# The Mamba-2 stage of a hybrid encoder layer: in-chunk products with the values as weights, states of the second direction first, outputs finished chunk by chunk in feature-major layout

## The chip, the cores and the metric

The kernel runs on one core of one Trainium2 chip. The metric is the device time of one launch in microseconds. TensorE (PE) multiplies, VectorE (DVE), ScalarE (ACT) and GpSimd (POOL) work elementwise, and the queues of SyncE (SP) and ScalarE issue the DMAs. Every engine takes its instructions in order. On TensorE a product of plain fp32 operands is two passes; in the profile each pass is one weight load (PEld) and one MATMUL.

## The reference

One layer: RMSNorm, one input projection (1024 to 10016 columns), three branches (Mamba-2 SSD, RWKV-7, HGRN2), a gated merge, an output projection, and a SwiGLU FFN. L = 1024 positions, all fp32. The change lies in the Mamba-2 branch: 16 heads of 64 values, 2 groups of 8 heads that share B and C of 128 states, chunks of 128 positions, two directions with decays of their own, summed:

```python
a_cum = jnp.cumsum(dt * a, axis=2)                       # within a chunk
lmat = jnp.exp(jnp.where(mask, a_cum[q] - a_cum[s], -inf))
cb = einsum('bcqgn,bcsgn->bcqsg', cm, bm)
y_diag = einsum('bcqsgh,bcsghp->bcqghp', cb[..., None] * lmat, x * dt)
chunk_states = einsum('bcsgn,bcsghp->bcghpn', bm, x * dt * exp(a_cum[-1] - a_cum))
# scan over chunks: S <- exp(a_cum[-1]) * S + chunk_states, prev = S before the chunk
y_off = einsum('bcqgn,bcghpn->bcqghp', cm, prev) * exp(a_cum)
y = y_forward + y_backward + x * d_skip
out = rmsnorm(y * silu(z), norm_w)                       # over all 1024 features
```

## The kernel before, in words

The layer runs rwkv, hgrn, `ssd`, then merges, output projection and FFN. The input projection is a list of jobs (`Jobs`), one for each tile of 128 columns, of 16 steps of three matmuls each (L329 to L331, `mm<-x`); `J.fill` and `J.share` put steps between the work of the branches, so that TensorE has something to do while the other engines prepare operands. `J.share(w)` issues that part of the remaining steps which weight `w` (from the list `FILL["ss"]`, called F) has in the remaining `J.weight`. The number of steps is the same whatever the weights are. Each job also casts and splits its weights (`wh` on ScalarE L220, `wl` on VectorE L222) and copies its result from PSUM and stores it (`st`, L271 and L272, on ScalarE and its queue). The tiles of z (`pz`) are jobs, as are the gates (`pg`), which are last.

`ssd` has two groups of 8 heads. For each, B, C and x are convolved (L1285 to L1289), the products CB of B and C are made for all chunks, and x is transposed so that positions are on the partitions (`xt`). Then a loop over i = 0 to 7 treats chunk i of the first direction and chunk 7 - i of the second:

- `pairs(c)` makes the in-chunk matrix of chunk c for 8 heads, 128 x 1024: for each direction a load that copies rows of cumulated decay (`cumd`) to all partitions (512 KB, in one of the EB = 5 buffers with tag E), a subtraction on POOL (L1357), then the choice between the directions by a mask (L1360, VectorE), exp (L1361, ScalarE) and the product with CB (L1362, VectorE). It runs two chunks ahead.
- For each direction: `yo`, the product of C with the state S (L1378, one matmul with 512 moving columns), scaled into `yt` (L1380) and added to Y on POOL (L1381); `xw`, the weighted values (L1384); `st`, their product with B (L1386); the state update, decay on POOL (L1390) and sum on VectorE (L1391).
- `yd`, the in-chunk products (L1397): for each head the 128 x 128 matrix as weights and 64 value columns as moving operand; the result is added to Y (L1399).
- Y starts as xt times `gd`, on POOL (L1371). `gd` holds the skip term and a diagonal term.

After the loop the group loads its four tiles of z, takes silu (L1408), transposes Y to features on partitions (`ytps`, L1417), multiplies (L1418), stores (`ysc`, L1419), and adds the squares to `ss` (L1425, L1426), which the last norm needs in the merge.

The order of the work on every engine but one is set by a planner, which takes what is ready in its own model of time, earlier program text first. POOL in the chunk loop keeps the program's order (`tc.manual_schedule(engines={POOL})`). Buffers of one tag are reused only when their last reader is through; DMAs of SP are issued in order, and one that waits holds back those behind it.

## Time and profile before

| | before |
|---|---|
| median of three runs | 2487.82 us (2487.3 to 2491.13) |
| profiled execution | 2489.66 us, its span 2487.9 us |
| busy share PE / DVE / ACT / POOL | 94% / 66% / 40% / 43% |
| granted TensorE clock, mean | 0.964 |
| bytes moved by DMA | 306.27 MB |
| chunk loop of the first group | about 1183 to 1283 us of the span |
| chunk loop of the second group | about 1376 to 1483 us |

Times in the answers are microseconds from the start of the span. A group of instructions is given by line, engine, operation and tiles (written <- read) with its shape and count, then busy time and mean duration of one in ns, then idle time of the engine before them and what ended it. The duration of a matmul reaches over the next one, since they are pipelined; the pace is read from one start to the next.

### The profile page before, as it was taken

Reading aid. Unit: us, or ns where it says so; the run is one execution under the profiler, and the core shown is the slowest. Engines: PE = TensorE matmul, PEld = TensorE weight load, DVE = VectorE, ACT = ScalarE, POOL = GpSimd, SP = SyncE. Lnnn points to the kernel's source line nnn. Section 1 sums busy time; section 2 is a strip of 40 time slices with the busy share of each in tenths; the row PEclk is TensorE's granted clock in tenths of the full one; section 3 lists DMA queues with packets and bytes.
Section 4 is the critical chain, followed back from the end, with each engine's and each line's share of the span. In section 5 each row is a group of like instructions: output and inputs, shape, how many; then the busy total and the mean of one; then the engine's idle time right before and its main releaser. Section 6 shows DMA issues by size and latency. Waiting matters only on the chain.

```text
span 2487.9 us, 37793 instructions
## 1 busy us (share of the span) xinstructions
PE 2332.5 (94%) x14785; PEld 1870.3 (75%) x14785; DVE 1635.9 (66%) x2130; ACT 988.9 (40%) x1460; POOL 1068.9 (43%) x862
## 2 busy tenths in 40 slices
PE   8998999999989889999899899999899999999995
PEld 6776788888867677778568667788688888877764
DVE  5688862456566866846666776553774454469999
ACT  6544532222464653436135235332433333344333
POOL 4433422344044533420751761421454444447885
PEclk9998999899999999999899999999999999999998
DMA  5455685655342232225645647531132222253321
GB/s 149 126 145 131 164 209 139 189 164 149 118 138 91 77 109 77 68 88 172 140 125 172 142 128 250 189 115 72 60 102 81 80 84 78 85 172 109 102 67 68
DMA packets 381215, 306.27 MB, mean 123 GB/s; under 512 B 111273, under 2 KB 323149, under 8 KB 381037
## 3 DMA queue, kind: packets, MB, share of 16 engines
q1 hardware_dynamic: 260909, 225.71, 30.6%
q10 hardware_dynamic: 119936, 77.61, 10.7%
q8 instruction: 117, 1.92, 0.3%
q0 software_dynamic: 192, 0.52, 0.1%
q14 instruction: 61, 0.50, 0.1%
HBM read 209.68 MB, written 94.11 MB: 122 GB/s over the span
## 4 chain that ended last, share of the span: by engine, by line
PE 59%; DVE 23%; POOL 5%; issue 5%; DMA 4%; ACT 3%; SPq 0%; ACTq 0%; DVEq 0%; POOLq 0%
PE mm L329 6%; PE mm L330 6%; PE mm L331 6%; PE ps L1577 6%; PE ps L1576 6%; PE ps L1578 6%; DVE acc L1915 3%; DVE ab L1793 2%; PE Gps L802 2%; PE mm L232 2%; PE mm L230 2%; PE mm L231 2%; DMA E<-cumd 2%; POOL E L1357 2%; DVE rb L1793 2%
## 5 line engine op out<-in xcount | busy, mean ns | idle before, releaser
L329 PE MATMUL mm<-x,wh 128*128 128x512 f32 (+1 forms) x1232 | 500.0, 406 | 0.5 <-ACT wh L220 0.5
L330 PE MATMUL mm<-x,wh 128*128 128x512 f32 (+1 forms) x1232 | 497.2, 404 | 0.0
L331 PE MATMUL mm<-x,wl 128*128 128x512 f32 (+1 forms) x1232 | 495.0, 402 | 0.8 <-DVE wl L222 0.7
L329 PEld LDWEIGHTS mm<-x,wh 128*128 128x128 f32 (+1 forms) x1232 | 234.5, 190 | 62.2 <-issue 10.6
L331 PEld LDWEIGHTS mm<-x,wl 128*128 128x128 f32 (+1 forms) x1232 | 234.7, 190 | 57.2 <-issue 6.0
L330 PEld LDWEIGHTS mm<-x,wh 128*128 128x128 f32 (+1 forms) x1232 | 234.8, 191 | 55.9 <-issue 6.8
L1577 PE MATMUL ps<-xb,rb 128*128 128x512 f32 x432 | 171.1, 396 | 0.0
L1576 PE MATMUL ps<-xb,rb 128*128 128x512 f32 x432 | 170.1, 394 | 0.0
L1578 PE MATMUL ps<-xb,rb 128*128 128x512 f32 x432 | 169.9, 393 | 0.0
L220 ACT CAST wh<-wr 128x1024 fp32r<-128x1024 f32 (+2 forms) x103 | 100.3, 974 | 125.1 <-PE mm L330 102.4
L222 POOL TENSOR_TENSOR wl<-wr,wh 128x1024 fp32r<-128x1024 f32 x30 | 78.2, 2606 | 149.2 <-ACT wh L220 140.0
L1576 PE MATMUL ps<-rb,ab 128*128 128x512 f32 x308 | 127.4, 414 | 14.3 <-DVE acc L1915 13.5
L222 DVE TENSOR_TENSOR wl<-wr,wh 128x1024 fp32r<-128x1024 f32 (+2 forms) x73 | 98.1, 1343 | 64.6 <-ACT wh L220 64.5
L1577 PE MATMUL ps<-rb,ab 128*128 128x512 f32 x308 | 125.3, 407 | 2.3 <-POOL rb L1793 2.3
L1578 PE MATMUL ps<-rb,ab 128*128 128x512 f32 x308 | 124.1, 405 | 1.5 <-DVE ab L1793 1.5
L1740 ACT CAST rb<-fs 128x512 fp32r<-128x512 f32 x85 | 52.5, 621 | 172.1 <-PE ps L1578 119.7
L271 ACT COPY st<-mm 128x512 f32<-128x512 f32 x130 | 75.5, 581 | 95.1 <-PE mm L331 76.0
L805 DVE TENSOR_TENSOR Gc<-Gps,mk 128x256 f32<-128x256 f32 x64 | 27.0, 423 | 112.4 <-PE Gps L802 58.6
L1576 PEld LDWEIGHTS ps<-xb,rb 128*128 128x128 f32 x432 | 81.2, 188 | 19.9
L1578 PEld LDWEIGHTS ps<-xb,rb 128*128 128x128 f32 x432 | 81.2, 188 | 19.0
L1577 PEld LDWEIGHTS ps<-xb,rb 128*128 128x128 f32 x432 | 81.1, 188 | 18.9
L1357 POOL TENSOR_TENSOR E<-E,cums 128x1024 f32<-128x1024 f32 x32 | 68.3, 2146 | 60.3 <-DMA E<-cumd 54.5
(503 smaller groups left out, 5584.8 us busy)
## 6 DMA issues: line engine op xcount, KB each, us to landing
wr<-in_w_in_dram ACTq DMA_DIRECT2D x74, 512.0 KB
fr<-in_ffn_w_in_dram SPq DMA_DIRECT2D x44, 512.0 KB
E<-cumd SPq DMA_DIRECT2D x32, 512.0 KB
pg<-st ACTq DMA_DIRECT2D x48, 256.0 KB
gt<-pg SPq DMA_DIRECT2D x24, 512.0 KB
ad<-a SPq DMA_DIRECT2D x22, 512.0 KB
dr<-in_ffn_w_down_dram SPq DMA_DIRECT2D x22, 512.0 KB
ar<-ad SPq DMA_DIRECT2D x22, 512.0 KB
```

Of the source, the lines that this page charges most:

```text
L220: nc.scalar.copy(hi[:, :kt, :n], raw[:, :kt, :n])
L222: g.lo_eng.tensor_sub(lo[:, :kt, :n], raw[:, :kt, :n], f32(hi[:, :kt, :n]))
L271: g.nc.scalar.copy(st[:n], ps)
L329: g.nc.tensor.matmul(ps[:n], w[0][:, k, :n], xh, start=(k == 0), stop=False)
L330: g.nc.tensor.matmul(ps[:n], w[0][:, k, :n], xl, start=False, stop=False)
L331: g.nc.tensor.matmul(ps[:n], w[1][:, k, :n], xh, start=False, stop=(k == KT - 1))
L1357: nc.gpsimd.tensor_tensor(e, e, cs.unsqueeze(2).broadcast_to([P, 8, P]), SUB)
L1576: nc.tensor.matmul(ps, ah, bh, start=(i == 0), stop=False)
L1577: nc.tensor.matmul(ps, ah, bl, start=False, stop=False)
L1578: nc.tensor.matmul(ps, al, bh, start=False, stop=(i == n - 1))
L1793: eng.tensor_sub(blk[:, 1], s, f32(blk[:, 0]))
L1915: nc.vector.tensor_add(m[j], m[j], ps)
```

## The change

- `yd`: the values `xt` (64 columns) are now the weights and the matrix `e` is the moving operand (128 columns), so that outputs come feature-major; the two heads of a 128-feature tile write the two halves of the partitions.
- `yo`: four products for each direction, the state's 128-column pieces as weights, C as the moving operand, also feature-major.
- The factor exp(a_cum) is no longer a table (`ecum`), but computed from the broadcast rows: X = Exp(e), in two instructions of 64 partitions for each direction, on ScalarE.
- The sign of `cums` is turned; for the first direction the addition to e is eight ScalarE instructions with a bias, for the second it stays one instruction on POOL.
- The diagonal and the skip term are put in the matrix by a second predicated copy on VectorE (`id8`, `gd`) in place of the POOL product that began Y.
- States of the second direction for all chunks come first (`Sb`, seven steps), and then a loop over chunks that finishes each: y = both X products + `yd`, times z, stored to `ysc`, square on ScalarE, square sums on POOL.
- z of the group is loaded, given silu and stored to a DRAM buffer `zd` ahead of the loop, through buffers of tag E, and reloaded chunk by chunk.
- The transposes `ytps` and the end-of-group work go. FILL weights are set anew: total 543 in place of 551.

The diff, cut to its core:

```diff
-    "ss": (4, 36, 12, 18, 6, 3, 8, 5, 22, 13, 8),
+    "ss": (4, 36, 14, 5, 7, 8, 22, 13, 6),
...
-    J.weight = F[8] + 2 * F[0] + F[9] + F[10] + 2 * (F[1] + 4 * F[2] + F[3] + 16 * F[4] + 8 * F[5] + F[6] + 4 * F[7])
+    J.weight = F[6] + 2 * F[0] + F[7] + F[8] + 2 * (F[1] + 4 * F[2] + 7 * F[3] + 8 * F[4] + 8 * F[5])
...
-            nc.vector.tensor_sub(cums, cums, ld)
+            nc.vector.tensor_sub(cums, ld, cums)
...
+                for q in range(grp * 4, grp * 4 + 4):
+                    zs = sp.tile([P, L + 4], F32, tag="E", name="zs", bufs=EB)[:, :L]
+                    nc.sync.dma_start(zs, J.get(g.pz, q))
+                    nc.scalar.activation(zs, zs, AF.Silu)
+                    nc.sync.dma_start(zd[q], zs)
...
                 def pairs(c):
-                        nc.gpsimd.tensor_tensor(e, e, cs.unsqueeze(2).broadcast_to([P, 8, P]), SUB)
+                        X = yp.tile([P, 4, P], F32, tag=f"X{d}", name="X", bufs=2)
+                        if c != (0, NT - 1)[d]:
+                            for b in range(2):
+                                hr = slice(b * 64, b * 64 + 64)
+                                nc.scalar.activation(X[hr], e[hr, b::2], AF.Exp)
+                        if d == 0:
+                            for h in range(8):
+                                nc.scalar.activation(e[:, h], e[:, h], AF.Identity, bias=cums[:, c, h0 + h:h0 + h + 1])
+                        else:
+                            nc.gpsimd.tensor_tensor(e, e, cums[:, c, h0:h0 + 8].unsqueeze(2).broadcast_to([P, 8, P]),
+                                                    ADD)
...
                     nc.vector.tensor_mul(e, e, CB[:, c:c + 1, :].broadcast_to([P, 8, P]))
+                    nc.vector.copy_predicated(e, id8.unsqueeze(1).broadcast_to([P, 8, P]),
+                                              gd[:, c].unsqueeze(2).broadcast_to([P, 8, P]))
...
+                def state(d, c, old, new):
+                    xw = yp.tile([P, 512], F32, tag="xw", name="xw", bufs=2)
+                    nc.vector.tensor_tensor(h3(xw), h3(xt[:, c]), per_head(wst, c, d), MUL)
+                    ps = pp.tile([P, 512], F32, tag="b", name="st", bufs=2)
+                    nc.tensor.matmul(ps, Bt[:, c], xw, start=True, stop=True)
+                    if old is None:
+                        nc.vector.tensor_copy(new, ps)
+                    else:
+                        nc.gpsimd.tensor_tensor(h3(new), h3(old), per_head(dec, c, d), MUL)
+                        nc.vector.tensor_add(new, new, ps)
...
-                nxt = [pairs(0), pairs(1)]
+                nxt = [pairs(0)]
+                for c in range(NT - 1, 0, -1):
+                    state(1, c, Sb[:, c] if c < NT - 1 else None, Sb[:, c - 1])
+                    J.share(F[3])
+                nxt.append(pairs(1))
                 for i in range(NT):
+                    z = yp.tile([P, 4, P], F32, tag="z", name="z", bufs=2)
+                    nc.sync.dma_start(z, zd[grp * 4:grp * 4 + 4, :, ts].rearrange("q p t -> p q t"))
+                    e, X = nxt.pop(0)
+                    part = []
+                    for d, S in ((1, Sb[:, i] if i < NT - 1 else None), (0, Sa if i else None)):
+                        if S is None:
+                            continue
+                        ps = pp.tile([P, 4, P], F32, tag="b", name="yo", bufs=2)
+                        for q in range(4):
+                            nc.tensor.matmul(ps[:, q], S[:, q * P:(q + 1) * P], CT[:, ts], start=True, stop=True)
+                        nc.vector.tensor_mul(X[d], X[d], ps)
+                        part.append(X[d])
+                    if i < NT - 1:
+                        state(0, i, Sa if i else None, Sa)
+                    J.share(F[4])
                     for h in range(8):
-                        nc.tensor.matmul(ps[:, h], e[:, h], xt[:, i, h * 64:h * 64 + 64],
+                        nc.tensor.matmul(ps[h % 2 * 64:h % 2 * 64 + 64, h // 2], xt[:, i, h * 64:h * 64 + 64], e[:, h],
                                          start=True, stop=True)
+                    y = part[0]
+                    if len(part) > 1:
+                        nc.gpsimd.tensor_add(y, y, part[1])
+                    nc.vector.tensor_add(y, y, ps)
+                    nc.vector.tensor_mul(z, z, y)
+                    nc.sync.dma_start(ysc[grp * 4:grp * 4 + 4, :, ts].rearrange("q p t -> p q t"), z)
+                    nc.scalar.activation(y, z, AF.Square)
+                    eng = nc.vector if grp and i == NT - 1 else nc.gpsimd
+                    eng.tensor_add(y[:, 0:2], y[:, 0:2], y[:, 2:4])
+                    if grp == 0:
+                        eng.tensor_add(ss[:, ts], y[:, 0], y[:, 1])
+                    else:
+                        eng.tensor_add(y[:, 0], y[:, 0], y[:, 1])
+                        eng.tensor_add(ss[:, ts], ss[:, ts], y[:, 0])
+                    if i + 2 < NT:
+                        nxt.append(pairs(i + 2))
                     J.share(F[5])
-                for q in range(4):
-                    zs = zss[q]
-                    for h in range(2):
-                        ps = pp.tile([P, 4, P], F32, tag="a", name="ytps", bufs=3)
...
```

More of the change, by code (lines that the diff above doesn't have):

```diff
@@ L1212, in ssd @@
         cums = kp.tile([P, NT, 32], F32, tag="cums", name="cums")
-        ecum = kp.tile([P, NT, 32], F32, tag="ecum", name="ecum")
         wst = kp.tile([P, NT, 32], F32, tag="wst", name="wst")
@@ L1228, in ssd @@
             nc.vector.tensor_scalar(dA, dt, an[:, 0:1], None, MUL)
-            J.share(F[8])
+            J.share(F[6])
             dtT = kp.tile([P, NT, 32], F32, tag="dtT", name="dtT")
@@ L1258, in ssd @@
             nc.scalar.activation(dec, pse, AF.Exp)
-            nc.scalar.activation(ecum, cums, AF.Exp)
             nc.vector.tensor_sub(wst, pse, cums)
@@ L1273, in ssd @@
                                 base=-1, channel_multiplier=1)
-        m8 = kp.tile([P, P], U8, tag="m8", name="m8")
+        m8, id8 = (kp.tile([P, P], U8, tag=n, name=n) for n in ("m8", "id8"))
         nc.vector.tensor_copy(m8, mlt)
+        nc.vector.tensor_copy(id8, g.ident)
         def conv(ct, dst):
@@ L1303, in ssd @@
                 conv(10 + grp, CT)
-                J.share(F[1] + F[9] * grp)
+                J.share(F[1] + F[7] * grp)
                 cbd = yp.tile([P, NT], F32, tag="cbd", name="cbd")
@@ L1343, in h3 @@
                     return t.rearrange("p (h v) -> p h v", v=64)
-                S = [yp.tile([P, 512], F32, tag=f"S{d}", name=f"S{d}") for d in range(2)]
-                J.share(F[3])
                 def pairs(c):
-                    Es = []
+                    Es, Xs = [], []
                     for d in range(2):
@@ L1353, in pairs @@
                         e = e[:, :L].rearrange("p (h t) -> p h t", t=P)
[L1354 to L1357 removed]
+                        h0 = d * 16 + grp * 8
+                        nc.sync.dma_start(e, cumd[h0:h0 + 8, c * P:(c + 1) * P].unsqueeze(0).broadcast_to([P, 8, P]))
+                        X = yp.tile([P, 4, P], F32, tag=f"X{d}", name="X", bufs=2)
[9 more added lines that the diff above has]
+                                                    ADD)
                         Es.append(e)
+                        Xs.append(X)
                     e = Es[0]
```

63 lines of the change are left out of this document (9 added, 54 removed).

## The prediction

> **What bounds the kernel now.** I read the page's engine line first, then windows over the two Mamba groups, the waits inside them, and single instructions. The windows show busy microseconds of each engine, then granted clock, DMA share and GB/s.
>
> ```profile
> PE 2332.5 (94%) x14785; PEld 1870.3 (75%) x14785; DVE 1635.9 (66%) x2130; ACT 988.9 (40%) x1460; POOL 1068.9 (43%) x862
> ```
> ```profile
> 1180.00:1300.00 120.00, 105.80 (x447) 75.73 (x446) 79.02 (x72) 30.36 (x35) 83.37 (x50) 0.93 0.52 130
> 1373.00:1493.00 120.00, 108.69 (x483) 79.37 (x482) 86.61 (x80) 33.66 (x41) 85.27 (x50) 0.96 0.55 138
> ```
> ```profile
> 1200.00:1220.00 20.00, 15.82 (x52) 10.49 (x52) 17.43 (x15) 3.65 (x4) 16.65 (x10) 0.62 0.38 84
> 1380.00:1400.00 20.00, 13.88 (x58) 10.07 (x57) 11.40 (x9) 1.06 (x1) 11.19 (x8) 0.74 0.65 160
> ```
> ```profile
> 1220.00:1260.00 40.00, 36.74 (x162) 25.95 (x161) 31.25 (x28) 5.54 (x7) 36.97 (x23) 1.00 0.64 142
> 1400.00:1440.00 40.00, 36.99 (x161) 26.26 (x161) 32.76 (x30) 7.04 (x9) 39.55 (x23) 1.00 0.64 136
> ```
>
> TensorE is the bound of the whole (94%), and what it does in the Mamba stage beside the stage's own products is filler: projection matmuls of later tiles. So the stage is worth its TensorE work plus TensorE's idle. The idle is 120 - 105.80 = 14.2 us in the first group and 120 - 108.69 = 11.3 us in the second, 25.5 us together. In the steady windows POOL is busy 36.97 and 39.55 of 40 us: POOL paces the chunks. VectorE has 80%, ScalarE 16%.
>
> ```profile
> PE yo L1378 <- DVE S L1388: 6.5, 1, 6.5
> POOL E L1357 <- DMA E<-cumd: 23.9, 4, 14.9
> ```
> ```profile
> 1393.27 2.08 PE L1378 MATMUL yo<-S,CT 128*128 128x512 f32 x2 [6.12 <-DVE S L1388]
> ...
> 1463.59 1.02 PE L1378 MATMUL yo<-S,CT 128*128 128x512 f32 x2
> ```
>
> The first two are waits of the first group (total, times, longest), the others instructions of the second (start, duration, idle before). Half the idle is one stall at each loop's start: the first copy of a state (L1388) sits on VectorE behind the second `pairs`, which waits for POOL, which waits for the broadcast load of `cumd`. Behind each stall the clock is low (0.62 and 0.74 in the windows; 2.08 us for a pair of passes that takes 1.02 later, so about half speed). (1 - 0.62) x 20 + (1 - 0.74) x 20 = 12.8 us is the most that this costs; if the 10.3 us of idle in these windows were all at half clock, 5.2 of it cost nothing, and 7.6 stay. I take 8. Idle and low clock: 33.5 us.
>
> **The change on TensorE.**
>
> ```profile
> 1385.27 1.89 PE L1397 MATMUL yd<-xt,E 128*128 128x64 f32 x16
> ```
> ```profile
> 1005.70 0.38 PE L1168 MATMUL ops<-sc,Vt 128*128 128x128 f32 x2
> ...
> 1008.15 0.39 PE L1170 MATMUL ops<-Eb,S 128*128 128x128 f32 x2
> 1008.30 0.48 PE L177 MATMUL nps<-t,ones 128*128 128x512 f32 x1
> ```
> ```profile
> 1071.15 1.15 PE L1075 MATMUL vps<-lv 128*64 128x64 f32 x32
> 1072.23 0.50 PE L331 MATMUL mm<-x,wl 128*128 128x512 f32 x1
> ```
> ```profile
> 1306.87 1.31 PE ytps L1417 x12
> ```
>
> In-chunk product `yd`: 8 products, two passes each; 1.89 us a chunk now (128 weight columns, 64 moving). After, 64 weight columns, 128 moving, outputs alternating between the upper and lower half of the partitions. A pass of 128 moving columns paces at (1008.30 - 1005.70) / 24 = 0.108 us when passes run one after another. The hgrn scores (L1075) already use 64-column halves: 32 passes of 64 columns in 1072.23 - 1071.15 = 1.08 us, 34 ns each, against 54 for half of 0.108; the halves overlap 1.6 times. Then 16 passes are 16 x 0.108 / 1.6 = 1.08 us, with a margin 1.15. Bounds: 1.73 without overlap, 0.87 with two full halves. Over 16 chunks: -11.8 us (bounds -2.6 and -16.3).
>
> The Trainium skill, "TensorEngine Tiling (Array Packing)", Key Properties, says that changing the tiling mode drains TensorE. It speaks against this step; the L1075 rows include one entry and one exit and agree that they are small. If each of some three pieces of `yd` cost 0.2 us for it, an estimate, the sum would be 9.6 us worse.
>
> The transposes `ytps` go: 64 at 1.31 / 12 = 0.109 us, -7.0 us. `yo` becomes four products of 128 moving columns each, two passes: 8 x 0.108 = 0.87 us; one 512-column product is 2 passes of four times 0.108, also 0.87. Zero, and nothing needs to hide it. State products are the same in number. TensorE work: -18.8 us.
>
> The fillers are conserved; only their weights move, and the z projections that are now read earlier are done by 1080 us anyway.
>
> ```profile
> 1117.00:1180.00 63.00, 53.48 (x226) 41.49 (x225) 0.00 (x0) 5.18 (x9) 1.00 0.54 173
> 1180.00:1300.00 120.00, 72.46 (x255) 47.77 (x254) 0.00 (x0) 6.33 (x11) 0.93 0.52 130
> 1300.00:1373.00 73.00, 65.94 (x284) 52.48 (x283) 0.00 (x0) 6.42 (x11) 1.00 0.53 170
> 1373.00:1487.00 114.00, 69.22 (x247) 45.31 (x246) 0.00 (x0) 6.34 (x11) 0.96 0.52 129
> L272 ACTq DMA_DIRECT2D pz<-st x16: 326/327/1585, 939.0 to 1075.5; - x16
> ```
> ```profile
> 1177.42 0.39 PE L329 MATMUL mm<-x,wh 128*128 128x512 f32 x1
> 1177.65 0.39 PE L330 MATMUL mm<-x,wh 128*128 128x512 f32 x1
> ```
>
> Four windows of the fillers alone hold 226 + 255 + 284 + 247 = 1012 matmuls at a start-to-start of 0.23 us, 229 us, or 0.42 us for each unit of the new weight 543. A new chunk has 15 units (6.3 us) + two `yo` and one `st` (2.6) + `yd` (1.15) = 10.05 us of TensorE. Each of the seven backward states has 5 units + 0.87 = 3.0 us. An old chunk had 5.4 + 15 units x 229/551 = 11.6 us and took about 13 (POOL).
>
> **POOL, ScalarE, VectorE, DMA per chunk.** Rows with count, busy us, mean ns:
>
> ```profile
> L1357 POOL TENSOR_TENSOR E<-E,cums 128x1024 f32<-128x1024 f32 x32 | 68.3, 2146 | 60.3 <-DMA E<-cumd 54.5 <-PE mm L331 5.7
> L1381 POOL TENSOR_TENSOR Y<-Y,yt 128x512 f32<-128x512 f32 x28 | 39.4, 1406 | 35.6 <-DVE yt L1380 35.6
> L1390 POOL TENSOR_TENSOR S<-S,dec 128x512 f32<-128x512 f32 x24 | 36.8, 1535 | 0.0
> L1371 POOL TENSOR_TENSOR Y<-xt,gd 128x512 f32<-128x512 f32 x16 | 25.6, 1620 | 0.0
> L839 POOL TENSOR_TENSOR S<-S,PC 128x256 f32<-128x256 f32 x30 | 18.4, 613 | 92.8 <-DVE SVc L838 91.6
> ```
>
> POOL now: 2 x 2.15 + 1.62 + 2 x 1.41 + 2 x 1.53 = 11.8 us. After: one E add, one decay, one `y` add and the square sums (0.61 for 256 columns, half for 128): 2.15 + 1.53 + 1.41 + 0.9 to 1.2 = 6.2 us. POOL stops being the bound. Its order is fixed by program order, so the E add of `pairs(0)` stands before the six decays of the backward states: these wait for its load.
>
> ```profile
> L1557 ACT ACTIVATE junk<-xn 128x512 f32<-128x512 f32 x16 | 9.6, 601 | 50.0 <-DVE xn L1555 50.0
> L1361 ACT ACTIVATE E<-E 128x1024 f32<-128x1024 f32 x16 | 17.0, 1061 | 130.5 <-DVE E L1360 130.5
> ```
>
> ScalarE gains four exponentials of 64 x 512 (4 x 0.60, as the square of 128 x 512), eight 128-column identities (1061 ns at 1024 columns and 601 at 512 leave about 0.14 + 0.12 at 128: 2.1 us; at most 8 x 0.60) and a square (0.6) beside its 1.06: 6.2 us, and with casts and copies of the fillers about 8 of 10. It fits, but those now queue behind instructions that wait for a load.
>
> ```profile
> L1360 DVE COPY_PREDICATED E<-m,E x16: 1316/2375/2410, 1189.3 to 1463.6; 128x1024 f32<-128x1024 uint8 x16
> L1384 DVE TENSOR_TENSOR xw<-xt,wst x28: 676/1522/2399, 1183.7 to 1468.8; 128x512 f32<-128x512 f32 x28
> L1362 DVE TENSOR_TENSOR E<-E,CB 128x1024 f32<-128x1024 f32 x16 | 24.1, 1506 | 2.8 <-ACT E L1361 2.8
> L1380 DVE TENSOR_TENSOR yt<-yo,ecum 128x512 f32<-128x512 f32 x28 | 19.1, 681 | 3.0 <-PE yo L1378 3.0
> L222 DVE TENSOR_TENSOR wl<-wr,wh 128x1024 fp32r<-128x1024 f32 x56 | 83.4, 1489 | 62.9 <-ACT wh L220 62.8
> ```
>
> VectorE after: two predicated copies (1.32 at least, 2.38 in the median, beside POOL), the CB product (about 1.2; 1.51), `xw` and the z product (0.68; 1.52 each), four with a PSUM operand (two X products, state add, y add: 0.68 each) and 0.6 of a filler's low part (0.9): 8.9 us undisturbed, 12.9 at today's medians. Today's chunk (one predicated copy, two `xw`, five with PSUM) holds 11.2 and loses 3.1 of it to POOL, which is busy 96%. With POOL at 6.2 of 11 (0.56), and a quarter more of VectorE's time open to it (6.1 for 4.8 us undisturbed), 3.1 x 0.56 / 0.96 x 1.27 is 2.3; with rounding I take 11.3 us. That is more than TensorE's 10.05: VectorE paces the new chunks, and TensorE idles 1.25 us in each, 20 us over 16 (now 3.26 + 3.01 in 80 us, about 1 in a chunk).
>
> The Trainium skill, "SBUF — State Buffer", Who interferes with whom, says the port pair of VectorE and POOL is an exclusive lock and the later instruction waits in full; 1316 against 2375 ns above agrees.
>
> ```profile
> q1 hardware_dynamic: 7836, 3.95, 46.9%
> ```
>
> DMA, from 40 us of the loop (1205 to 1245): 46.9% x 40 x 16 / 7836 = 38 ns for a 512-byte packet. A pair of E loads is 2048 packets, 4.9 us of all 16 engines. New in each chunk: z in and y out in 512-byte runs, 512 packets and 1.2 us each. With 0.63 of a weight load (1024 packets: 1.5) and the fillers' stores (I put half of that, 0.8): 9.6 us, against 0.64 busy today. The SP queue issues in order; a y store that waits for VectorE holds the loads behind it.
>
> Start of the loop: z now goes through the five E buffers (load, silu, store) before `pairs(0)`, so E comes some microseconds later, but seven states with 21 us of TensorE work need no E. I leave 4 us a group of stall and low clock: 8 us, where 12.6 + 8 stood. The moved silus cost nothing on ScalarE (40% busy) if two table loads stay two. The end-of-group z work and 4 us of transposes fall away.
>
> **Sum**, against the profiled execution of 2489.66 us (span 2487.9 + 1.8; the median of the runs is 1.8 below it, so I make no correction larger than that): work -18.8; idle 33.5 to 20 + 8 = 28, -5.5; total -24.3, hence 2465 us; 2464 with half the difference to the median taken off.
>
> **Rivals.** (1) Slower: VectorE keeps today's medians (12.9) and is held at 0.9 of a chunk by its own waits (0.80 today): 14.3 us. The change breaks even when idle is 33.5 + 18.8 = 52.3 us, that is (52.3 - 8) / 16 = 2.8 us a chunk, a chunk of 12.8. 14.3 gives 2489.7 + 1.5 x 16 = 2514. For it: 1.52 us as the median of `xw`. Against: POOL does half. Chance 0.13. (2) DMA paces: 9.6 us at a share of 0.8 is 12.0 (2477), at 0.75 12.8 (no change). For it: 23.9 us of POOL's waits are for E. Against: E can be loaded a chunk ahead. Chance 0.17. (3) VectorE is freed along with POOL: chunks at TensorE's pace with 0.3 us idle, start stalls 3: 2489.7 - 18.8 - 33.5 + 8 = 2445. For it: ScalarE's room. Chance 0.2. (4) The column halves do not overlap: `yd` 1.73, a chunk of 10.6, still below VectorE's; +0 to 9 us, 2464 to 2473. Chance 0.05 by itself. My forecast, 2452 to 2475: 0.45.
>
> 0.2% of this time is 5 us, about what can be told from no change. Faster: 0.45 + 0.2 + 0.05 + two thirds of (2) = 0.82; same 0.05; slower 0.13. The range runs from rival 3 to just above no change, 2440 to 2492; the likeliest case alone 2452 to 2475.
>
> **What would show it.** Right: `yd` rows of 16 passes near 1.1 us; no transposes after the loop; POOL near 0.55 and VectorE above 0.9 in the steady windows; the 6 us wait at each loop start gone. Wrong: chunk periods above 12.8 us; waits for E or z loads on ScalarE and POOL; a DMA share above 0.85; fillers on TensorE waiting for ScalarE's copies.

## The result and the profile after

The changed kernel is slower: 2533.41 us (2529.31 to 2536.53) against 2487.56 (2485.99 to 2491.13), a ratio of 1.018, interval 1.0165 to 1.0195: 46 us lost where 24 were forecast to be won. The profiled execution took 2536.53 us, its span 2534.5; that of before took 2489.66. Ahead of the Mamba stage, where the edits change at most the order of filler, executions differ too: between 440 and 560 us the granted clock was 0.94 in the traces of before and after and 1.00 in four of those below (late, x3, all2, before_yd), which reach the stage some 4 to 9 us sooner.

The engine line of the page, after:

```profile
PE 2322.8 (92%) x14889; PEld 1866.9 (74%) x14889; DVE 1619.7 (64%) x2150; ACT 1064.2 (42%) x1652; POOL 1011.8 (40%) x846
```

Where the time went is read from a few milestones: the last transpose of x (`xps`), the first and the last `yd` of each group's loop, and the first matmul of the next stage (`mm<-oh`, L230). The rows are answers of the timeline for one line of code in one stretch: count, min/median/max ns, first and last start. Before:

```profile
L1334 PE MATMUL xps<-ident,xq x32: 270/272/273, 1163.6 to 1183.2; 128*128 128x128 f32 x32
L1397 PE MATMUL yd<-xt,E x128: 217/275/421, 1193.6 to 1285.0; 128*128 128x64 f32 x128
L1334 PE MATMUL xps<-ident,xq x32: 270/272/273, 1346.3 to 1375.9; 128*128 128x128 f32 x32
L1397 PE MATMUL yd<-xt,E x128: 217/275/421, 1385.3 to 1472.2; 128*128 128x64 f32 x128
L230 PE MATMUL mm<-oh,wh x144: 387/389/792, 1483.7 to 1599.9; 128*128 128x512 f32 x144
```

After:

```profile
L1334 PE MATMUL xps<-ident,xq x32: 270/272/275, 1164.0 to 1183.9; 128*128 128x128 f32 x32
L1420 PE MATMUL yd<-E,xt x128: 272/273/323, 1220.1 to 1338.7; 128*64 128x128 f32 x128
L1334 PE MATMUL xps<-ident,xq x32: 270/272/273, 1355.3 to 1385.6; 128*128 128x128 f32 x32
L1420 PE MATMUL yd<-E,xt x128: 272/273/473, 1420.3 to 1525.2; 128*64 128x128 f32 x128
L230 PE MATMUL mm<-oh,wh x92: 389/389/796, 1526.8 to 1599.3; 128*128 128x512 f32 x92
```

| us | before | after |
|---|---|---|
| first group: last `xps` to first `yd` | 10.4 | 36.2 |
| first `yd` to last (7 chunks on) | 91.4 | 118.6 |
| second group: last `xps` | 1375.9 | 1385.6 |
| to first `yd` | 9.4 | 34.7 |
| first `yd` to last | 86.9 | 104.9 |
| last `yd` to next stage | 11.5 | 1.6 |

The next stage begins 43.1 us later: x of the second group is 9.7 late, its loop starts 25.3 later still, lasts 18.0 longer, and the work behind the loop is 9.9 shorter. The first group's loop ends 53.7 us later, but only 9.7 of this reach the second group: TensorE is busy for 101.63 of that loop's 118.6 us, since it holds 288 filler matmuls. A measure that leaves out what happened earlier is called the stage time below: from the last `dps<-q,t` product of hgrn, the branch ahead (at 1034.3 before and 1034.6 after), to the first `mm<-oh`, 449.4 us before and 492.2 after. The windows over the stage say the same for TensorE. Before, then after:

```profile
1180.00:1483.70 303.70, 278.20 (x1238) 208.65 (x1236) 203.14 (x187) 93.81 (x112) 175.25 (x115) 0.96 0.53 139
```
```profile
1180.00:1526.80 346.80, 273.59 (x1375) 210.14 (x1373) 202.00 (x212) 176.19 (x314) 116.52 (x101) 0.90 0.61 156
```

TensorE's busy time fell a little and POOL's by a third, VectorE's stayed, and ScalarE's rose from 93.81 to 176.19 us. TensorE's idle time rose from 25.5 to 73.2 us, and the clock went from 0.96 to 0.90 with it. By stretches, the first loop, the start of the second and the second loop (windows of after):

```profile
1220.10:1338.70 118.60, 101.63 (x546) 78.34 (x546) 80.45 (x82) 60.31 (x110) 52.91 (x42) 0.93 0.62 148
...
1385.60:1420.30 34.70, 30.80 (x121) 22.82 (x119) 15.92 (x18) 22.58 (x46) 7.39 (x5) 0.95 0.87 202
1420.30:1525.20 104.90, 59.15 (x341) 43.69 (x340) 62.08 (x68) 48.37 (x88) 49.69 (x42) 0.79 0.49 126
```

The first start (1183.9 to 1220.1, 30.79 us busy) idles 5.4 us, the first loop 17.0, the second start 3.9 and the second loop 45.8, where before it idled 11.1 of 86.9. So the loss of TensorE's time lies in the second loop, and there at its end (windows of after):

```profile
1460.00:1480.00 20.00, 3.03 (x25) 1.88 (x24) 4.18 (x6) 10.85 (x15) 4.88 (x6) 0.67 0.86 191
1480.00:1500.00 20.00, 10.63 (x58) 7.60 (x60) 14.13 (x16) 13.31 (x28) 9.38 (x8) 0.71 0.41 93
1500.00:1520.00 20.00, 6.87 (x46) 4.87 (x43) 11.05 (x12) 7.59 (x15) 13.14 (x12) 0.72 0.24 65
...
1477.00:1515.00 38.00, 16.23 (x94) 11.21 (x94) 23.42 (x25) 22.81 (x45) 21.23 (x19) 0.72 0.37 92
```

From 1477 to 1515, three chunks, no engine is busy for more than 62% of the time, and DMA is at 0.37. Yet a chunk takes 12.7 us, as POOL's timeline shows (start, duration, idle before and its releaser):

```profile
1490.10 1.89 POOL L1367 TENSOR_TENSOR E<-E,cums 128x1024 f32<-128x1024 f32 x1 [1.38 <-ACT X L1362]
1491.95 1.04 POOL L1391 TENSOR_TENSOR Sa<-Sa,dec 128x512 f32<-128x512 f32 x1
1492.95 2.29 POOL L1424 TENSOR_TENSOR X<-X 128x512 f32<-128x512 f32 x1
1499.62 0.73 POOL L1431 TENSOR_TENSOR X<-X 128x256 f32<-128x256 f32 x1 [4.38 <-ACT X L1429]
1500.43 0.45 POOL L1435 TENSOR_TENSOR X<-X 128x128 f32<-128x128 f32 x1
1500.96 0.45 POOL L1436 TENSOR_TENSOR ss<-ss,X 128x128 f32<-128x128 f32 x1
1502.79 1.89 POOL L1367 TENSOR_TENSOR E<-E,cums 128x1024 f32<-128x1024 f32 x1 [1.38 <-ACT X L1362]
```

The steps between two E additions are on the other engines (timeline of after, VectorE's and ScalarE's rows):

```profile
1492.03 2.12 DVE L1372 COPY_PREDICATED E<-m,E 128x1024 f32<-128x1024 uint8 x1 [1.23 <-POOL E L1367]
...
1494.18 1.06 ACT L1373 ACTIVATE E<-E 128x1024 f32<-128x1024 f32 x1 [4.15 <-DVE E L1372]
1495.27 1.28 ACT L1362 ACTIVATE X<-E 64x512 f32<-64x512 f32 x2
1496.58 2.45 ACT L1365 ACTIVATE E<-E,cums 128x128 f32<-128x128 f32 x8
1498.93 0.61 ACT L1429 ACTIVATE X<-z 128x512 f32<-128x512 f32 x1
1501.45 1.27 ACT L1362 ACTIVATE X<-E 64x512 f32<-64x512 f32 x2 [1.90 <-POOL ss L1436]
```

This is a ring. The E addition (1.89 us) releases VectorE's choice by the mask (2.12), and this releases ScalarE's list, which runs in order: the Exp of the matrix (1.06), an Exp of X for the next chunk but one (1.28), its eight identities (2.45) and the Square (0.61). POOL adds the squares in the tile X (three additions, 1499.62 to 1501.41); the second Exp of X (1.27) needs that tile, because X has two buffers; and the next E addition needs this Exp, because E is changed in place. Added up, that is 12.5 of the 12.69 us, with no step idle in between. Beside it runs a path of the same length on POOL: the state's decay and the sum of the directions (L1424), which frees the tile of the first Exp of X, end at 1495.24, just as ScalarE comes to this Exp (1495.27). z is ready at 1497.71; the Square starts only at 1498.93, behind the identities.

A second cause is seen where 20 us hold only 3.03 us of TensorE. The planner has put the gates of the next stage into the loop (timeline of after):

```profile
1457.09 10.64 SPq L1486 DMA_DIRECT2D gt<-pg  x4
...
1461.97 1.28 ACT L1487 ACT_TABLE_LOAD   x1
...
1472.10 1.06 ACT L1487 ACTIVATE gt<-gt 128x1024 f32<-128x1024 f32 x1 [8.85 <-DMA gt<-pg]
...
1481.85 2.05 PE L1412 MATMUL yo<-CT,Sa 128*128 128x128 f32 x8 [18.67 <-DVE Sa L1392]
```

ScalarE waits 8.85 us for a gate with the loop's Exp behind it, and TensorE 18.67 us for a state. In the first loop the next group's convolution stands in the same way: ScalarE waits 8.44 us for its load (L1285, 1315.53), and TensorE 13.53 us for a state.

### The profile page after: what moved, and what is told of

Same layout as the page of the kernel before. It is cut to its first block, busy times and chain, and to the rows that moved or that the text cites. A ratio compares the mean times of both kernels' runs of the same rounds, so it can differ in the third digit from the quotient of the medians.

```text
span 2534.5 us, 38264 instructions
## 1 busy us (share of the span) xinstructions
PE 2322.8 (92%) x14889; PEld 1866.9 (74%) x14889; DVE 1619.7 (64%) x2150; ACT 1064.2 (42%) x1652; POOL 1011.8 (40%) x846
## 5 line engine op out<-in xcount | busy, mean ns | idle before, releaser
L222 DVE TENSOR_TENSOR wl<-wr,wh 128x1024 fp32r<-128x1024 f32 (+2 forms) x73 | 90.7, 1243 | 74.0 <-ACT wh L220 74.0
L230 PE MATMUL mm<-oh,wh 128*128 128x512 f32 x224 | 89.2, 401 | 7.8 <-DVE gt L1496 4.3
```

The lines of the kernel that those rows point to most:

```text
L222: g.lo_eng.tensor_sub(lo[:, :kt, :n], raw[:, :kt, :n], f32(hi[:, :kt, :n]))
L230: nc.tensor.matmul(ps, whi[:, k, :n], xh, start=(k == 0), stop=False)
```

## Experiments

Four theories went in. Latency (L): the ring above paces the chunks. Intruders (I): the next stage's instructions in the loop. VectorE (V): its added work. DMA (D): the traffic of z. The ratios are to the kernel before, run on the same chip in the same job; the changed kernel's is 1.018, and 0.001 is 2.5 us. Runs whose interval holds 1.018 are not told apart from the changed kernel. Beside the ratio stands the stage time (492.2 us in the changed kernel), from one execution each.

**hold: next stage behind the loop.**

```diff
+                    g.hold_act = nc.scalar.activation(y, z, AF.Square).ins   # and hold_sp, the last z load
...
+                if b == 1 and f < 4:                   # gates; the same for conv 9 and 11
+                    held.enter_context(g.tc.issue_after(g.hold_sp))
+                    held.enter_context(g.tc.issue_after(g.hold_act))
```

> The changed kernel with one thing more: the first activations and loads of the next stage (the next group's convolution of B and C; the first four gate tiles of the merge) are queued on ScalarE and SP behind the loop's last square and last z load. Changed kernel: about 2533 us. Theory L (one chunk's path round POOL, ScalarE and VectorE, 12.7 us a chunk, is longer than TensorE's work, and fillers run out): the two long waits for Sa (13.5 and 18.7 us) shrink to the loop's own 3 to 7 us, but chunks keep 12.7 us; 2510 to 2525. Theory I (the intruders are the loss): both waits go with the low clock behind them, 2495 to 2505. Theory V (VectorE's own work is the bound) and theory D (DMA traffic is the bound): no change, 2528 to 2538.

2516.75 us, ratio 1.0121 (1.0066 to 1.0175), stage time 478.0. TensorE's waits for the state fall from 57.2 us in 9 to 36.4 in 8, the longest from 18.7 to 6.7 us (waits of the run, 1200 to 1527 us: total, times, longest), and the second loop lasts 96.2 us in place of 104.9:

```profile
PE yo L1418 <- DVE Sa L1398: 36.4, 8, 6.7
```

I is shown by the waits, for some 15 us; the size is uncertain, since the interval overlaps the changed kernel's own (1.0165 to 1.0195). Without the intruders the ring stays: E additions still start at 1446.71, 1459.72, 1472.74 and 1485.42 us, 12.7 to 13.0 apart, which is L's picture.

**early: the next chunk's E and X ahead of Square and sums.** `pairs(i + 2)` stands before the Square, which gets a tile of its own.

> The changed kernel, but the square goes to a tile of its own (so that X is free after z's product), and the preparation of chunk i+2 is placed ahead of the square and the square sums of chunk i. L: a chunk loses the sums (1.8 us), the square (0.6) and ScalarE's wait before it (1.2) from its path, 12.7 to about 9 to 10.5 us, so 2490 to 2510. I: the intruders stay, 2525 to 2535. V and D: no change.

2525.94, ratio 1.0157 (1.0105 to 1.021), stage time 487.3: within what the changed kernel may be, and L's forecast of 2490 to 2510 missed. The sums still stood in POOL's order between the E addition and the decay.

**nopred: the second predicated copy on VectorE left out** (no diagonal and skip term).

> The changed kernel without the second predicated copy on VectorE (leaves out the diagonal's own value and the skip term). V: 16 x 1.3 to 2.2 us less on the bound, 2500 to 2513. L: the copy is off the path of a chunk (it comes after z's product), 2525 to 2535. I and D: 2525 to 2535.

2529.02, ratio 1.017 (1.0117 to 1.0222), stage time 494.2: taking 16 x 1.3 us of work off VectorE shows no gain, and the 20 to 33 us that V forecast are outside the interval. V falls. The copy is no step of the ring.

**nozd: z read raw**, with no silu and no trip through `zd`.

> The changed kernel with z read chunk by chunk from the projection's own buffer (leaves out silu of z), so no load, silu and store of z ahead of the loop and 8 MB less of DMA. D: 8 MB at 200 GB/s is 40 us of DMA engines, of which a good part would come back, 2500 to 2515. L and I: only the stalls at the loops' starts (4.3 and 3.9 us and the low clock behind them) shrink, 2520 to 2532. V: 2528 to 2538.

2514.27, ratio 1.0111 (1.0065 to 1.0156), stage time 476.2, inside D's range (2500 to 2515) and below that of L and I (2520 to 2532). The loops start 13.0 and 28.6 us sooner (timeline of the run):

```profile
L1417 PE MATMUL yd<-E,xt x128: 272/273/323, 1207.1 to 1327.5; 128*64 128x128 f32 x128
L1417 PE MATMUL yd<-E,xt x128: 272/273/476, 1391.7 to 1508.1; 128*64 128x128 f32 x128
```

The preparation of z is a large part of what delays the loops: from the last `xps` to the first `yd` are now 23.5 and 18.2 us, where the changed kernel has 36.2 and 34.7 and the kernel before 10.4 and 9.4. D has a point here: the DMA share is 0.76 and 0.87 in the changed kernel's two starts. But the second loop then lasts 116.4 us, 11.5 longer: part of the gain is given back.

**yadd: the sum of the directions on VectorE.**

```diff
-                        nc.gpsimd.tensor_add(y, y, part[1])
-                    nc.vector.tensor_add(y, y, ps)
+                    nc.vector.tensor_add(y, y, ps)
+                        nc.vector.tensor_add(y, y, part[1])
```

> The sum of the two directions (y + part, 2.29 us on POOL, 14 times) goes to VectorE as a second SBUF addition of about 0.69 us behind the one that takes yd. The theory of the loop's latency (one chunk is a closed chain of 12.7 us, in which POOL's addition stands): each chunk that the chain paces gets about 1.6 us shorter, so some 12 x 1.6 = 20 us, 2533 -> about 2513, and POOL's E additions of the second group stand about 11 us apart. The theory that VectorE paces the chunks: 14 x 0.69 = 10 us more work there, about 2543. The theory of the next stage's instructions in the loop alone: no change, 2528 to 2537.

2524.94, ratio 1.0163 (1.0125 to 1.02), stage time 484.9: no sure change, and not the 20 us that were forecast for a closed chain with this addition in it. By the rows above, a path of the same length that doesn't hold it stands beside it.

**late: Square and sums one chunk later**, `pairs(i + 2)` right behind z's product.

> Square goes to a tile of its own, the next-but-one chunk's E and X stand right behind z's product, and the Square and the sums of a chunk are issued one chunk later, behind y's addition. The loop's latency: sums (1.63 us on POOL) and the wait for Square (about 2.5 us behind the identities) leave the chain, 12.7 -> about 10 us a chunk: 12 x 2.5 = 30 us less, about 2503. The theory of the next stage's instructions alone: 2528 to 2537. VectorE paces: no change.

2517.21, ratio 1.0131 (1.0102 to 1.0161): 12 us better, under half of what L forecast. Its trace doesn't show the gain where L puts it: E additions of the second loop are 10.7 to 13.8 us apart, the loop lasts 107.7 us, and the stage time is 486.3, 5.9 less than in the changed kernel; 8.7 us of its lead stand ahead of the stage, where the clock was 1.00.

**pin: filler tied to the second loop.**

```diff
+                    if self.pin is not None:           # the last yd matmul of the chunk before
+                        held.enter_context(g.tc.issue_after(self.pin))
```

> In the second group's loop the projection matmuls (filler) that the program places behind chunk i may not be issued ahead of chunk i's last yd matmul; nothing else is changed. In the order of instructions about 39 of them (39 x 0.227 = 8.9 us) then stand in every chunk, where the changed kernel has none behind its third chunk and the more ahead of the loop. The theory that the filler ran out: TensorE's idle time and low clock of 1440 to 1545 us (about 45 us) is filled from the 60 us ahead of the loop, and the loop starts that much sooner: about 2495 (2485 to 2508). If the chain of the loop is no longer than what the filler covers anyway, or the part ahead of the loop is bound by ScalarE and VectorE and not by filler: 2520 to 2535. The next stage's ScalarE instructions still sit in the loop, so a wait of over 10 us stays.

2533.51, ratio 1.0197 (1.0165 to 1.023). TensorE is now busy through the loop and idle ahead of it instead (windows of the run, from the last `xps` to the first `yd` and from there to the last):

```profile
1381.90:1415.80 33.90, 11.84 (x14) 3.19 (x13) 11.80 (x14) 19.15 (x40) 6.93 (x5) 0.55 0.77 185
1415.80:1516.20 100.40, 96.93 (x537) 76.67 (x538) 67.78 (x73) 48.01 (x92) 50.11 (x43) 0.97 0.52 140
```

First and last `yd` are at 1415.8 and 1516.2, little before the 1420.3 and 1525.2 of the changed kernel. The start takes 33.9 us without any filler and took 34.7 with it, so filler doesn't set it. The loop holds 282 filler matmuls in place of 83 and is now paced by TensorE itself (96.93 of 100.40 us). Filler that is moved into this loop is thus no gain at this amount. The bare start shows why it takes so long (timeline of the run):

```profile
1401.20 1.89 POOL L1371 TENSOR_TENSOR E<-E,cums 128x1024 f32<-128x1024 f32 x1 [39.52 <-ACT X L1366]
...
1405.87 3.92 PE L1391 MATMUL st<-xw,Bt 128*128 128x512 f32 x4 [16.05 <-DVE Sb L1396]
```

POOL waits for the Exp of a load of E that is queued with z's stores; the decays of the second direction stand behind that addition, and TensorE waits 16.05 us for them.

**pin_hold: both.**

> Both: filler tied to the chunks of the second loop, and the next stage's loads and first activations held behind the loop. If the two are separate causes their gains add: 2533 - 17 - 38 = about 2478 (2465 to 2492), on the fast side of the kernel before. If the one covers the other: 2495 to 2517.

2529.85, ratio 1.0182 (1.0148 to 1.0216), stage time 485.3: hold's gain does not show. The loop holds the same 282 filler matmuls, TensorE is busy for 96.42 of its 100.0 us (1407.7 to 1507.7), and what filler was left stood between loop and next stage (1516.9).

**stfirst: the states ahead of `pairs(0)`; x3: a third buffer for X**, whose room comes from BT, put into E's ring.

> The second direction's seven states stand ahead of pairs(0) in the program, so that POOL's order, which is written out, has the six Sb decays ahead of the first E addition. In the trace of the run with the filler tied to the loop, the first decay stood 16 us behind that addition, which waited for a DMA of E, while the PSUM of the states was ready. The theory of the loop's start: the states end about 16 us sooner and E's path sets the start, about 8 us sooner in each group, 2533 - 16 = about 2517 (2510 to 2524). If E's load sets the start in either order: 2527 to 2537.

> X gets three buffers in place of two (the room comes from BT, which goes into E's ring of five buffers), so that the Exp of the next-but-one chunk no longer waits until Square and sums have left X. The loop's latency by X's buffers: the chunks that the chain paces (some five of the second group, some of the first) lose the Exp's wait, 12.7 -> about 11 us, 10 to 15 us in all: about 2520. If POOL's written order closes the chain by itself: no change, 2527 to 2537. A loss, if the ring of E is now too short for the convolution: up to 2545.

2539.31, ratio 1.02 (1.017 to 1.0229), and 2539.35, ratio 1.02 (1.0148 to 1.0252). Both miss. With the states first, the E addition stands behind the decays, and the first `yd` comes at 1233.7 and 1432.5, later than 1220.1 and 1420.3. With X's third buffer the E additions no longer wait for the Exp, and the last three of the second loop are 11.8 and 11.0 us apart (1503.94, 1515.74 and 1526.72 us), as forecast for a ring without this step; but those before are 14.7 to 18.1 apart, and x of the second group is 8.3 us later (1393.9 in place of 1385.6). BT in E's ring, which also carries the convolution, may be the reason; it was not tried alone.

**all: late, hold, stfirst and the second group's z early; all_x3: with X's third buffer.**

> Together: Square and sums one chunk later in a tile of their own (alone -16), the next stage's loads and first activations held behind the loop (alone -17), the states ahead of pairs(0) (expected -16), and the second group's silu of z ahead of its x convolution, so that its 4 MB do not stand before E's loads (the run without that round trip gave -19 for both groups; for one some -10). If the stage is one chain end to end, they add: 2533 - 59 = about 2474 (2462 to 2490). If they open the same idle time: 2495 to 2510.

> The same with X's three buffers. By the loop's latency some 10 us below the run without (about 2464); if POOL's order closes the chain anyway, the same as that run within 5 us.

2511.71, ratio 1.0093 (1.0064 to 1.0122), stage time 473.7, and 2528.0, ratio 1.0154 (1.0125 to 1.0184). The forecast sum missed because its term for stfirst was wrong: late, hold and stfirst as they were measured alone (12 and 15 us better, 5 worse) add up to 22 us, which is what `all` has. The third buffer, forecast at 10 us better or the same, made it some 15 us worse. In the chain of `all` (start, duration, what) the long pieces are now transfers: a z load waits until a y store has landed, and a load of E stands behind it on the same queue:

```profile
1462.48 10.76 DMA ysc<-z
...
1473.29 0.36 SPq L1431
...
1473.75 8.61 DMA E<-cumd
```

**z4: z in four buffers; zearly2: z's preparation of both groups ahead of the x convolution**, and the first group's z projected sooner.

> z gets four buffers in place of two (BT's 4 KB become two tiles of the same ring). A z load then no longer waits for the y store of two chunks before, and the E loads behind it on SyncE's queue go out at once. The theory of the queue: the changed kernel showed 47 us of waits for y stores in the first loop, of which what reaches TensorE is some 10 to 20 us in both: about 2518 (2510 to 2525). If E's loads were early enough in any case: 2529 to 2537.

> The silu of z of each group stands ahead of its x convolution, and the projections of the first group's z ahead of those of the second group's x. Its 4 MB then do not stand before E's first loads. The run without the round trip gained 19 us at the loops' starts; if it was its place that cost this, as much comes back here: about 2515 (2508 to 2522). If the traffic itself costs wherever it stands: 2527 to 2537.

2525.73, ratio 1.0142 (1.0113 to 1.0172), stage time 486.0: some 9 us better by the ratio and 6 by the stage time. SP's z loads still wait for y stores, 32.2 us in place of 47.1 between 1200 and 1340 us, and the second loop is not shorter (110.1 us). That the queue gives these us is not shown. 2532.68, ratio 1.017 (1.0128 to 1.0213): z's place alone is worth nothing. The loops start at 1217.1 and 1418.4, hardly sooner, because the x transposes ahead of them now end at 1200.0 and 1393.2, later than 1183.9 and 1385.6. What in z's trip costs nozd's 17 us was not separated further.

**all2: late, hold, z4, zearly2.**

> Square and sums later, next stage held behind the loop, silu of z early in both groups, z in four buffers; the states again behind pairs(0). The run of the earlier four together was 2512, with 22 us of its idle time at 1462 to 1484 us and 12 us at 1212 to 1228 us behind SyncE's queue. If these are the rest, some 25 us come back: about 2485 (2475 to 2495), level with the kernel before. If the loop's own chain of about 11 us stays behind them: 2500 to 2512.

2507.24, ratio 1.0068 (1.0044 to 1.0092), stage time 468.9: the best of the new form, 28 us better than the changed kernel by the ratios and still slower than before. Its first `mm<-oh` comes at 1499.1, 15.4 us after that of before, and its trace is among those that were ahead of the stage by some us. Its ring has lost the Square and the sums (timeline of the run, POOL's, VectorE's and ScalarE's rows):

```profile
1451.78 1.90 POOL L1380 TENSOR_TENSOR E<-E,cums 128x1024 f32<-128x1024 f32 x1 [1.99 <-ACT X L1375]
1453.70 2.12 DVE L1385 COPY_PREDICATED E<-m,E 128x1024 f32<-128x1024 uint8 x1 [1.25 <-POOL E L1380]
1455.92 1.06 ACT L1386 ACTIVATE E<-E 128x1024 f32<-128x1024 f32 x1 [3.57 <-DVE E L1385]
1456.96 1.28 ACT L1375 ACTIVATE X<-E 64x512 f32<-64x512 f32 x2
1458.26 2.44 ACT L1378 ACTIVATE E<-E,cums 128x128 f32<-128x128 f32 x8
1460.62 1.25 ACT L1375 ACTIVATE X<-E 64x512 f32<-64x512 f32 x2
1461.94 1.89 POOL L1380 TENSOR_TENSOR E<-E,cums 128x1024 f32<-128x1024 f32 x1 [1.98 <-ACT X L1375]
```

From one E addition to the next are 10.16 us, where the changed kernel had 12.69. The Square and the sums took the 2.52 us from 1498.93 to 1501.45 there, and 12.69 - 2.52 = 10.17: these steps are gone from the ring and nothing else, which shows L's mechanism. The third addition follows after 10.17 us, at 1472.11; the one behind it waits 6.61 us for a load. POOL's own list of a chunk is done 1.98 us before the Exp that the E addition waits for. Only its part up to the sum of the directions can pace the loop: that ends at 1456.93, again just as ScalarE comes to the Exp of X.

**all3: all2 and yadd; all3_pin: with 21 filler matmuls tied to each chunk.**

> The last run's edits together (2507) and the sum of the directions on VectorE, which takes 2.25 us from POOL's list of 10.2 us a chunk. If POOL's list is the loop's bound: E additions of the second loop about 8 us apart, some 8 chunks x 2.2 = 15 to 20 us less: about 2490 (2482 to 2497). If VectorE (16 of 20 us in that loop) takes over as the bound: 2500 to 2510.

> The same with filler tied to the second loop's chunks, 21 matmuls (4.8 us) a chunk, and fewer ahead of the loop. If what stands ahead of the loop waits for TensorE behind filler, the loop starts sooner and is covered: 10 to 15 us less than all3, about 2478 (2470 to 2488). If the chain ahead of the loop sets its start, as it did in the changed kernel: the same as all3 within 5 us.

2523.55, ratio 1.0136 (1.0115 to 1.0157), and 2522.27, ratio 1.013 (1.0115 to 1.0145). Taking 2.25 us off POOL's list came out 17 us slower by the ratios (stage times 480.8 and 468.9), and filler tied to the chunks changed nothing, as forecast for a chain ahead of the loop. Windows over uncovered chunks of all2, then of all3:

```profile
1441.00:1482.00 41.00, 22.09 (x123) 14.58 (x123) 33.63 (x36) 21.99 (x46) 32.35 (x24) 0.83 0.78 173
```
```profile
1437.00:1472.00 35.00, 19.04 (x126) 13.93 (x126) 31.59 (x33) 20.81 (x45) 21.14 (x17) 0.80 0.46 115
```

VectorE goes from 82% to 90% while POOL drops from 79% to 60%, and the E additions stay 10.2 to 11.3 us apart. Taking POOL's sum of the directions off opens one of two paths of equal length; the other, by way of the mask and ScalarE's list, stays, and the sum now stands in VectorE's list with the mask. The two loops are 3.7 and 4.2 us longer (106.5 and 96.0 in place of 102.8 and 91.8); the rest is spread over the parts between them and behind, and 3 us lie ahead of the stage. The runs do not explain it.

**before_yd: the in-chunk product alone, in the kernel before.**

```diff
-                        nc.tensor.matmul(ps[:, h], e[:, h], xt[:, i, h * 64:h * 64 + 64],
+                        nc.tensor.matmul(ps[h % 2 * 64:h % 2 * 64 + 64, h // 2], xt[:, i, h * 64:h * 64 + 64], e[:, h],
```

> The kernel before with the one edit that its in-chunk product takes the values as weights (16 products of 128x64 weights and 128 moving columns, in the place of 16 of 128x128 weights and 64 columns). Its PSUM tile is then feature-major and is added to the time-major Y as it stands, so that the layout of this summand is wrong and only the time can be read. If TensorE paces that loop (88.33 of 95.00 and 84.81 of 90.00 us busy): 16 x (1.89 - 1.15) = 11.8 us less, 2490 - 12 = about 2478 (2474 to 2482). If the loop's chain over POOL and VectorE paces it: 2485 to 2492.

2494.8 us against 2488.44, ratio 1.0026 (1.0016 to 1.0035). The product itself is as cheap as forecast (timeline of the run):

```profile
1408.77 1.09 PE L1397 MATMUL yd<-E,xt 128*64 128x128 f32 x16
```

but the time is outside both forecast ranges, some 6 us longer. The profiled execution was the shortest of eleven (2486.72), and its trace shows why: at the last `xps` of the first group it is 7.2 us ahead of before (1176.0 against 1183.2), in a part that the edit doesn't touch and where the clock was 1.00. In the stage the loops are 2.1 and 4.1 us shorter (89.3 and 82.8 us), but the parts ahead of, between and behind them are 4.6 longer, and from that `xps` to the first `mm<-oh` are 298.9 us in place of 300.5. So 1.6 of the 11.8 us are kept: most of this work was not on the path even in the loop as it was. From there to the end are 1010.1 us in place of 1004.2. That is where this trace loses; the same part takes 1001.7 to 1010.1 us in the traces of all kernels here, and no run says why.

## Why the prediction was wrong

**Right: TensorE's work.** `yd` was put at 1.15 us a chunk, and is (timeline of after):

```profile
1451.60 1.09 PE L1420 MATMUL yd<-E,xt 128*64 128x128 f32 x16
```

The halves overlap, since 16 passes one after another would be 1.73 us, and the switch of the tiling mode costs little, as the trace of before suggested; the drain of which the Trainium skill ("TensorEngine Tiling (Array Packing)", Key Properties) speaks is inside these 1.09 us. TensorE's busy time on the page falls by 9.7 us (2332.5 to 2322.8) and not by 18.8: products behind a wait run at a low clock, so that `yo` and `st` take 5.7 us more in the stage than before. No transposes follow the loop: last `yd` to next stage is 1.6 us. POOL's 6.2 us a chunk and ScalarE's 8 of 10 were near: from 1410 to 1527 us POOL is busy 53.20 and ScalarE 58.68 us, 6.7 and 7.3 for each of eight chunks (windows of after):

```profile
1410.00:1527.00 117.00, 68.36 (x367) 49.74 (x368) 71.82 (x80) 58.68 (x110) 53.20 (x45) 0.79 0.52 129
```

**Wrong first: "the stage is worth its TensorE work plus TensorE's idle"**, with the idle taken over from before. It is true as an account, but the two are not independent: before_yd took 11.8 us of work away, the stage shortened by 1.6, and the time did not fall. In a loop that another chain paces, work taken from TensorE comes back as idle.

**The step that failed: "VectorE paces the new chunks", 11.3 us, and with it the 20 us of idle in the loops.** They idle 62.7 us, 17.0 in the first, of which 13.5 are the wait at the convolution, and 45.8 in the second. VectorE needs 71.82 / 8 = 9.0 us a chunk, less than forecast: only the choice by the mask, beside POOL, is slow (2.12 us), and the second copy takes 1.30. nopred shows that VectorE does not pace. The step added up each engine's work and took the largest sum; it never followed one chunk through the engines. The ring POOL, VectorE, ScalarE, POOL, ScalarE gives 12.7 us with every engine at 62% or less, and the gates come on top: the second loop has 104.9 / 7 = 15.0 us a chunk. (The first has 118.6 / 7 = 16.9, but 14.5 of that is TensorE's work, filler above all.) Before, POOL was near 100% in the steady windows, so that a sum of work was near the pace; with POOL relieved, the latency of one chunk was next.

**Right in the idle, wrong in what it bought: "4 us a group of stall" at the loops' start.** TensorE idles 5.4 and 3.9 us there. But the starts take 36.2 and 34.7 us where 10.4 and 9.4 stood. The seven states were moved there; the prediction named what holds them up (z through the E buffers, the decays behind `pairs(0)` on POOL) and took it as hidden by the states' 21 us of TensorE work, while that work itself waits for the decays. TensorE's gap was covered by 104 and 107 filler matmuls.

**Wrong: "15 units" of filler, 6.3 us, in each new chunk.** 288 filler matmuls stand in the first loop, 83 in the second, and none in its last five chunks. The planner takes filler when its model sees a gap. By pin and all3_pin, moving it back shows no gain, because the second start is about as long without it (33.9 and 34.7 us in pin and the changed kernel).

**Not foreseen: the next stage's gates and convolution in the loop**, some 15 us by hold.

Rival 1 had the sign, with another mechanism (VectorE's medians). Rival 2 (DMA paces) is not what the slow chunks of 1480 to 1520 us show, with shares of 0.24 to 0.41; but the second loop's start has 0.87, and nozd, without z's traffic, wins some 17 us. Of the signs named for a miss, chunk periods above 12.8 us (15.0 in the second loop), waits for E loads (ScalarE, 8.2 us at the longest) and a DMA share above 0.85 (that start, and 0.86 from 1460 to 1480 us) came; filler waiting for ScalarE's copies did not.

Open stay: which part of z's trip costs nozd's 17 us, why yadd on top of all2 lengthens the stage, where before_yd's 6 us come from, and whether the new form can reach the old time at all; the best run lacks 17 us.

## What to carry to other kernels

Cost a loop twice: each engine's work per step, and the chain of one step through the engines up to the point where the next may begin, including written orders, in-place updates and buffers that are reused. In a trace, follow one instruction to its next turn: the steps that come without a gap between them are the ring, and only a step that leaves it shortens the pace. Here the Square and its sums did (12.69 to 10.16 us); VectorE's second copy, which stands beside it, did not, nor did POOL's sum of the directions, which has a path of equal length beside it. Where filler covers a loop, a saving on the engine that is busiest may be worth nearly nothing, and one edit alone in the old loop tells so cheaply. Compare traces from a milestone just ahead of the edit: here up to 9 us of difference came from a part that no edit touched.

## What the runs showed of the hardware

In these traces TensorE's clock is low where it idles: 0.71 and 0.72 in the windows of 1480 to 1520 us, where it is busy 10.63 and 6.87 of 20 us, and 0.97 in pin's loop, where it is busy 96.93 of 100.40. The eight `yo` products of a direction take 1.05 us in an unbroken row (1447.67 us) and 2.05 behind the 18.67 us of idle. A gate in the loop costs ScalarE more than its own 1.06 us: a table load of 1.28 us goes with each change between the gates' function and the loop's Exp, four between 1461.97 and 1481.62 us.
